# The odd mixer's 31-tap convolution: two of its four channel chunks on TensorE, and the LayerNorm between the output products

## The chip, the cores and the metric

The kernel runs on one core of a Trainium2 chip. The metric is device time in microseconds (us), the median of the timed runs; the profile shows one more execution of the same program, taken by the hardware profiler. The engines are TensorE (PE; its weight loads have rows of their own, PEld), VectorE (DVE), ScalarE (ACT), GpSimd (POOL) and SyncE (SP), whose queue issues the transfers of weights. "Granted clock" is the share of full speed that the chip's throttle gave TensorE.

## The reference

Two layers of a decoder trunk, 512 tokens, 1024 channels, all in float32, each a mixer and a gated ConvFFN with residual sums, then a final norm. The first layer's mixer is the even one (retention and a state-space scan), the second's the odd one, and only the odd mixer is touched:

```python
proj = h @ w_in                                  # h: the normed x, 1024 channels
ca, cg, u = split_cols(proj, [512, 512, 512])
c = ca * sigmoid(cg)                             # GLU
c = causal_dwconv(c, conf_dw_w, conf_dw_b)       # 31 taps, each channel by itself
c = silu(layer_norm(c, conf_ln_g, conf_ln_b))    # over the 512 channels
s = gelu(s5_ssm(u, ...))                         # 32 groups of 16 channels, 64 complex states each
s = s * sigmoid(s @ s5_glu_w)
return concatenate([c, s]) @ w_out               # 1024 -> 1024, added to x
```

## The kernel before

**Tiles.** x lies as 8 chunks of 128 channels (on the partitions) by 512 tokens. A projection to 128 output channels is a loop over the chunks of its input, and each step is three products of 128x512 (`mm3`, L98 to 101): the rounded weight with the rounded input (L99), with the input's remainder (L100), and the weight's remainder with the rounded input (L101). A weight comes through `wload` (L83): a transfer on SP's queue to `wraw` (4 buffers, L88), the rounded copy `whi` on ScalarE (3 buffers, L89), and the remainder `wlo` on VectorE (3 buffers, L90), or on another engine if the caller names one. The input of a projection is split in the same way (L94 on ScalarE, L95 on VectorE). The projections accumulate in one pool of four PSUM banks, all else in a second pool of four. What is not a weight lives in a pool of 56 slots of 128x512.

**Order.** A scheduler orders each engine's instructions by the order in which the program issues them and by what each depends on; `issue_after` and `high_priority` change that in a few places. Each engine runs its own list in order, so an instruction that waits holds up all behind it.

**The odd mixer** (`odd`, L817) issues, in this order:

1. `glu_in(i)`, for the four chunks of convolution channels: the projections pca and pcg (24 products each), on VectorE their products with R (the norm's reciprocal root, L836 and L837), a sigmoid on ScalarE, the gated product, and on ScalarE the first tap with the bias (L842). Of the other 30 taps, `POOLTAPS` gives all of chunk 0 and 20 of chunk 3 to GpSimd, a product and a sum each (L850 and L851), so that chunk 3 has two partial sums.
2. `s5_state(q)`, for the four chunks of S5 channels: the projection pu, whose weight's remainder is made on GpSimd; its product with R (uf, L872); transposes (pu2, puT); the input products pS (L893, 128x64 float32, 16 of them, alternately to the lower and upper 64 partitions); and on VectorE the S5 rotation (L897 to L917), to the states sst.
3. `s5_y(q)`: the output products pY with the kernels `toep` (L931) and `w2` (L933), two banks of PSUM one after the other, both on the lower 64 partitions, and copies on ScalarE (L935). `s5_gelu`: transposes (pyT, L942) and the GELU (L944). `out_loads` brings toep and w2 through SP's queue (L968, L969).
4. The S5 gate: projections pgl, sigmoid, product, split.
5. The output projection over the S5 half, po (8 output chunks of 12 products), each added to x on VectorE (L1010).
6. The taps that are left to VectorE (`conv`, L861): 30 each for chunks 2 and 1, 10 for chunk 3. The scheduler puts them wherever VectorE's list has room. Then the partial sums of chunk 3 are added.
7. The LayerNorm over channels: transposes of the convolution to tokens on the partitions (pLN, L1024), statistics (L1025), root and scaling (ln, L1039 and L1041), transposes back (pLNT, L1046), SiLU (lnc, L1048), split.
8. The output projection over the convolution half, po again (L1056 adds it to x), and with it the next norm's sums.

Of the kernel before, what the change touches and what calls it, by code (L numbers as in the profile page):

```python
# [15 lines left out]
P = 128  # L16
# [9 lines left out]
NPAIR = SH // 2  # L26
POOLTAPS = {0: range(1, 31), 3: range(11, 31)}
WV0 = (0, 1, 3, 6)
# [7 lines left out]
class Trunk:  # L36
# [21 lines left out]

    # ---------------------------------------------------------------- helpers
    def unpack(self, name, items, eng):  # L60
# [108 lines left out]

    # ---------------------------------------------------------------- ConvFFN  # L170
    def ffn(self, l, st, nxt, aside=None, out=None):
# [41 lines left out]
        if out is None:  # L213
            return nst
        # the last channels by halves of the tokens, so that the first half leaves under the second
        c = KC - 1
# [70 lines left out]

    # ---------------------------------------------------------------- even mixer
    def even(self, st):
# [13 lines left out]

        # values of the first head and dt, tokens on the partitions
        mm = nc.tensor.matmul
# [21 lines left out]

        # dt
        bc = lambda t: t.unsqueeze(1).to_broadcast(CH)
# [142 lines left out]

        # retention
        cosR, sinR = self.slot("cosR"), self.slot("sinR")
# [135 lines left out]

    # ---------------------------------------------------------------- S5 parameters
    def s5_prep(self):
# [16 lines left out]
        with self.tc.issue_after(self.dma_mark.ins), self.tc.issue_after(self.add_mark.ins):  # L629
# [87 lines left out]
            cmul(bbr, bbi, b(fr), b(fi), br, bi, bt)  # L717
            # powers by descending exponent: qr[., j] = a^(7-j); the same for a^(8-j)
            pw2_ = self.slot("s5p2")
# [11 lines left out]
            eng.memset(zt, 0.0)  # L731
            # chunk rotation e^(i 8 theta k) and the decay |a|^8
            cur = (co, si)
# [81 lines left out]

    # ---------------------------------------------------------------- odd mixer
    def odd(self, st):  # L817
# [8 lines left out]
        def glu_in(i):  # L826
            pa = self.pp("pca")
            self.proj(pa, ins["wca"][i], xs)
            pg = self.pp("pcg")
            self.proj(pg, ins["wcg"][i], xs)  # L830
            if "R" not in st:
                self.norm_end(st)
            R = st["R"]
            a = self.tp.tile([P, T], F32, name="cp", tag="cp", bufs=2) if i in POOLTAPS else self.slot("ca")
            b = self.tmp("cg")
            V(a, pa, R, op=ALU.mult)  # L836
            V(b, pg, R, op=ALU.mult)  # L837
            nc.scalar.activation(b, b, AF.Sigmoid)
            V(a, a, b, op=ALU.mult)
            cin[i] = a  # L840
            o = self.slot(f"cv{i}")
            nc.scalar.activation(o, a, AF.Identity, scale=kw[:, i, 30:31], bias=kb[:, i:i + 1])  # L842
            cv[i] = o
            pa = o
            if i in POOLTAPS and len(POOLTAPS[i]) < 30:
                pa = self.slot("cvp")
                nc.gpsimd.memset(pa, 0.0)
            for s in POOLTAPS.get(i, ()):
                t = self.tp.tile([P, T], F32, name="prod", tag="prod", bufs=1)
                nc.gpsimd.tensor_scalar(t, a, kw[:, i, 30 - s:31 - s], 1.0, op0=ALU.mult, op1=ALU.mult)  # L850
                nc.gpsimd.tensor_tensor(pa[:, s:], pa[:, s:], t[:, :T - s], op=ALU.add)  # L851
            cvp[i] = pa
# [10 lines left out]

        us, sst = {}, {}

        def s5_state(q):
            p = self.pp("pu")
            self.proj(p, ins["wu"][q], xs, eng=nc.gpsimd)
            if "R" not in st:
# [52 lines left out]
        def s5_y(q):  # L922
            y2 = [self.slot("y2")[:64].rearrange("p (i x) -> p i x", i=4) for _ in range(2)]
            for b in range(2):
                tp_, w2 = outw[q][b]
                p = self.ps("pY")
                for gl in range(4):
                    g = 4 * b + gl
                    ks = slice(g * 64, g * 64 + 64)
                    o = p[:64, gl * P:(gl + 1) * P]  # L930
                    mm(o, lhsT=us[q][:, ks], rhs=tp_.rearrange("p (i g c) -> p i g c", i=8, g=4)[:, :, gl, :],  # L931
                       start=True, stop=False)
                    mm(o, lhsT=sst[q][:, ks], rhs=w2[:, gl * P:(gl + 1) * P], start=False, stop=True)  # L933
                for e in range(2):
                    nc.scalar.copy(y2[e].rearrange("p i (g c) -> p g i c", c=16)[:, 4 * b:4 * b + 4],  # L935
                                   p[:64].rearrange("p (g i c) -> p g i c", g=4, i=8)[:, :, 4 * e:4 * e + 4])
            return y2
# [41 lines left out]
        s5_loads(0)  # L979
        glu_in(1)  # L980
        s5_loads(1)
        s5_state(0)
        s5_state(1)
        s5_loads(2)
        s5_loads(3)
        s5_state(2)
        s5_state(3)
        for q in range(4):
            out_loads(q)
        glu_in(2)  # L990
        y2[0] = s5_y(0)
        glu_in(3)
        for q in range(1, 4):
            y2[q] = s5_y(q)
            s5_split(q - 1)
        s5_split(3)
        mix = [None] * 8
        for m in range(4):
# [7 lines left out]
            mix[4 + m] = (hi, lo)  # L1006
        for c in range(KC):
            p = self.pp("po")
            self.proj(p, ins["woo"][c, :, 4 * P:], mix[4:])
            V(self.x[c], self.x[c], p, op=ALU.add)  # L1010
        conv(2)
        conv(1)
        conv(3, range(1, 4), ev[3])
        conv(3, range(4, 11), ev[4])
        for i in range(4):
            if cvp[i] is not cv[i]:
                V(cv[i], cv[i], cvp[i], op=ALU.add)
        bs, mv = self.small("bs4", [P, NT, 4, 6], 1), self.small("mv", [P, NT, 2])
        pt = [self.ps("pLN") for _ in range(NT)]
        for i in range(4):  # L1020
            with self.tc.issue_after(self.mark.ins), self.tc.high_priority() if i < 3 else nullcontext():
                for t in range(NT):
# [13 lines left out]
        for t in range(NT):  # L1036
# [3 lines left out]
            else:  # L1040
                nc.vector.tensor_scalar(z, pt[t], rs[:, t:t + 1], nm[:, t:t + 1], op0=ALU.mult, op1=ALU.add)  # L1041
            zs.append(z)
        for i in range(4):
            p = self.ps("pLNT")
# [15 lines left out]

# ---------------------------------------------------------------- host layout
def wtiles(w):
    k, m = w.shape
    return w.reshape(k // P, P, m // P, P).transpose(2, 1, 0, 3).reshape(m // P, P, k)


def chunks(v):
    return np.moveaxis(v.reshape(-1, P, *v.shape[1:]), 1, 0)
# [16 lines left out]
def layout(i):  # L1085
# [26 lines left out]
    o["wu"] = wtiles(w[:, 1024:])  # L1112
    o["wgl"], o["woo"] = wtiles(n["o_glu_w"][0]), wtiles(n["o_w_out"][0])
    c["kw"], c["kb"] = chunks(n["o_dw_w"][0].T), chunks(n["o_dw_b"][0])
    c["lg"], c["lb"] = chunks(n["o_ln_g"][0]), chunks(n["o_ln_b"][0])
# [43 lines left out]
```

## Time and profile before

| | |
|---|---|
| timed runs, us | 1402.01, 1399.62, 1400.68; median 1400.68 |
| profiled execution, first to last instruction, us | 1400.0 |
| busy, us (share) | PE 1331.6 (95%), PEld 1104.2 (79%), DVE 991.1 (71%), ACT 547.9 (39%), POOL 299.2 (21%) |
| mean granted clock of TensorE | 0.969 |
| traffic of the transfers | 143.00 MB |

For the profiled execution only its span is given; the timed runs are the measure of the time. The odd mixer lies about from 810 to 1035 us of the span. How to read the rows shown further down: a row of a stretch has its bounds and length, then for each engine in turn the busy time with the count of instructions, the granted clock, the transfers' busy share and GB/s. A group's row has the line, the engine, the operation, the tiles out<-in, shapes, the count, then busy time, the mean length of one in ns, and after a second bar the idle time of the engine just before. A single row begins with its start and its length in us; what stands in square brackets is the engine's idle time before it and what ended that.

### The profile page before, as it was taken

To read this page: it belongs to the slowest core of one execution; us is meant where nothing else is said; L and a number is where in the kernel's file an instruction comes from. 1 tells how busy PE (TensorE), PEld (TensorE's weight loads), DVE (VectorE), ACT (ScalarE), POOL (GpSimd) and SP (SyncE) were. 2 spreads that over 40 slices of the span, in tenths; PEclk is the share of its full clock that TensorE was granted. 3 is DMA by queue.
4 is the path that set the end of the run, shared out by engine and by line. 5 is a ranking of instruction groups with operands and counts; after the bars stand their busy time and mean duration, and the time that the engine had idled before them with its cause. 6 is when DMAs were issued, how large, how long until landed. Compare 5 with 4: busy or idle time off the path is not lost.

```text
span 1400.0 us, 17171 instructions
## 1 busy us (share of the span) xinstructions
PE 1331.6 (95%) x6468; PEld 1104.2 (79%) x6468; DVE 991.1 (71%) x1573; ACT 547.9 (39%) x769; POOL 299.2 (21%) x420
## 2 busy tenths in 40 slices
PE   8999999999999899999999987968799999999997
PEld 7788888888887778888888865756588888888887
DVE  6887777688578998777533369999887777774333
ACT  5455444444353334444322221143444444443221
POOL 0210010002009446800000059769000000000100
PEclk9999999999999999999999997888899999999999
DMA  6432232231244434532333332401142333232321
GB/s 218 153 121 69 75 113 91 90 105 64 90 142 121 124 95 139 177 106 87 98 98 94 106 113 83 143 16 53 62 134 94 103 91 106 90 97 88 102 75 61
DMA packets 48803, 143.00 MB, mean 102 GB/s; under 512 B 6352, under 2 KB 7680, under 8 KB 48720
## 3 DMA queue, kind: packets, MB, share of 16 engines
q1 hardware_dynamic: 42560, 124.34, 28.0%
q0 software_dynamic: 5872, 17.37, 4.3%
q8 instruction: 51, 0.84, 0.2%
q14 instruction: 32, 0.26, 0.1%
q10 hardware_dynamic: 288, 0.19, 0.0%
HBM read 131.88 MB, written 9.99 MB: 101 GB/s over the span
## 4 chain that ended last, share of the span: by engine, by line
PE 78%; DVE 17%; issue 2%; POOL 2%; ACT 1%; DMA 0%; DVEq 0%; ACTq 0%; POOLq 0%
PE pup L101 10%; PE pup L99 10%; PE pup L100 10%; PE pdn L101 6%; PE pdn L99 6%; PE pdn L100 6%; DVE cv L861 3%; DVE wlo L90 3%; PE po L99 2%; PE po L101 2%; PE po L100 2%; DVE ffa L189 1%; PE pxbc L100 1%; PE pxbc L99 1%; PE pxbc L101 1%
## 5 line engine op out<-in xcount | busy, mean ns | idle before, releaser
L89 ACT CAST whi<-wraw 128x1024 fp32r<-128x1024 f32 (+3 forms) x246 | 231.0, 940 | 492.5 <-PE pup L100 131.5
L90 DVE TENSOR_TENSOR wlo<-wraw,whi 128x1024 fp32r<-128x1024 f32 (+3 forms) x242 | 272.7, 1128 | 137.6 <-ACT whi L89 137.5
L101 PE MATMUL pup<-xh,wlo 128*128 128x512 f32 x704 | 276.1, 392 | 9.0 <-DVE wlo L90 9.0
L99 PE MATMUL pup<-xh,whi 128*128 128x512 f32 x704 | 276.5, 393 | 0.0
L100 PE MATMUL pup<-xl,whi 128*128 128x512 f32 x704 | 275.2, 391 | 0.0
L101 PEld LDWEIGHTS pup<-xh,wlo 128*128 128x128 f32 x704 | 133.1, 189 | 38.2 <-DVE wlo L90 10.1
L100 PEld LDWEIGHTS pup<-xl,whi 128*128 128x128 f32 x704 | 133.2, 189 | 27.7
L99 PEld LDWEIGHTS pup<-xh,whi 128*128 128x128 f32 x704 | 133.2, 189 | 27.3
L189 DVE SCALAR_TENSOR_TENSOR ffa<-ffh,c,ffa 128x511 f32<-128x511 f32 (+1 forms) x176 | 149.8, 852 | 2.9
L99 PE MATMUL pdn<-acth,whi 128*128 128x512 f32 (+1 forms) x374 | 140.9, 377 | 0.0
L100 PE MATMUL pdn<-actl,whi 128*128 128x512 f32 (+1 forms) x374 | 140.8, 377 | 0.0
L101 PE MATMUL pdn<-acth,wlo 128*128 128x512 f32 (+1 forms) x374 | 140.8, 377 | 0.0
L184 DVE TENSOR_TENSOR ffh<-pup,R 128x512 f32<-128x512 f32 x88 | 60.5, 687 | 63.6 <-PE pup L101 63.3
L231 POOL TENSOR_SCALAR x<-x,c 128x512 f32<-128x512 f32 (+1 forms) x9 | 9.3, 1034 | 402.0 <-ACT acc L127 302.9
L186 ACT ACTIVATE ffa<-ffh,c 128x512 f32<-128x512 f32 x88 | 71.9, 817 | 49.5 <-DVE ffh L184 47.3
L100 PEld LDWEIGHTS pdn<-actl,whi 128*128 128x128 f32 x374 | 70.4, 188 | 12.9
L101 PEld LDWEIGHTS pdn<-acth,wlo 128*128 128x128 f32 x374 | 70.4, 188 | 12.9
L99 PEld LDWEIGHTS pdn<-acth,whi 128*128 128x128 f32 x374 | 70.4, 188 | 12.8
L100 PE MATMUL po<-ml,whi 128*128 128x512 f32 x192 | 76.5, 399 | 3.8 <-DVE ml L95 3.8
L99 PE MATMUL po<-mh,whi 128*128 128x512 f32 x192 | 76.2, 400 | 0.5 <-ACT mh L94 0.5
L101 PE MATMUL po<-mh,wlo 128*128 128x512 f32 x192 | 76.3, 397 | 0.1
L94 ACT CAST acth<-ffg 128x512 fp32r<-128x512 f32 x44 | 27.3, 621 | 106.7 <-DVE ffg L196 104.4
(424 smaller groups left out, 2436.3 us busy)
## 6 DMA issues: line engine op xcount, KB each, us to landing
wraw<-in_wup_dram SPq DMA_DIRECT2D x88, 512.0 KB, 3.5
wraw<-in_wdn_dram SPq DMA_DIRECT2D x32, 512.0 KB, 3.5
wraw<-in_weo_dram SPq DMA_DIRECT2D x32, 256.0 KB, 3.0
wraw<-in_wxbc_dram SPq DMA_DIRECT2D x12, 512.0 KB, 3.7
wraw<-in_wdn_dram SPq DMA_DIRECT2D x16, 384.0 KB, 3.1
wraw<-in_wz_dram SPq DMA_DIRECT2D x8, 512.0 KB, 3.4
wraw<-in_wg_dram SPq DMA_DIRECT2D x8, 512.0 KB, 3.7
ar<-acd POOLq DMA_DIRECT2D x16, 256.0 KB, 4.0
```

Source lines behind the costliest of these rows:

```text
L89: nc.scalar.copy(hi[:, :n], raw[:, :n])
L90: (eng or nc.vector).tensor_tensor(lo[:, :n], raw[:, :n], hi[:, :n].bitcast(F32), op=ALU.subtract)
L94: self.nc.scalar.copy(hi, src)
L99: mm(out, lhsT=w[0], rhs=x[0], start=start, stop=False)
L100: mm(out, lhsT=w[0], rhs=x[1], start=False, stop=False)
L101: self.mark = mm(out, lhsT=w[1], rhs=x[0], start=False, stop=stop)
L184: nc.vector.tensor_tensor(h, p, st["R"], op=ALU.mult)
L186: nc.scalar.activation(a, h, AF.Identity, scale=dw[:, j, 2:3], bias=db[:, j:j + 1])
L189: nc.vector.scalar_tensor_tensor(a[:, s:], h[:, :T - s], dw[:, j, tap:tap + 1], a[:, s:], op0=ALU.mult, op1=ALU.add)
L231: self.nc.gpsimd.tensor_scalar(self.x[c][:, ts], self.x[c][:, ts], st["g"][:, c:c + 1], 1.0, op0=ALU.mult, op1=ALU.mult)
L861: nc.vector.scalar_tensor_tensor(a[:, s:], cin[i][:, :T - s], kw[:, i, 30 - s:31 - s], a[:, s:], op0=ALU.mult, op1=ALU.add)
```

## The change

The convolution's chunks 2 and 3 move to TensorE. With taps j = 0, 2, ... 30 as 16 shifts, one product takes two taps: its input `cx` holds 64 channels of the gated product on one half of the partitions and the same channels, one token later, on the other half; its weight `kd` has the two taps on two diagonals of 64x64. A chunk is two halves g of 64 channels, so 32 products, which the code issues with the halves alternating, each half to its own 64 partitions of one bank (pcv). The copy that is one token late is made on ScalarE, and ScalarE adds the bias when it takes the result from PSUM. The kernels come from a new input array through SP's queue. Chunk 0 stays on GpSimd and chunk 1 on VectorE; GpSimd loses its 20 taps of chunk 3 and the remainders of the pu weights, which go to VectorE.

Beside that the order changes: glu_in(1) stands behind the first s5_state; glu_in(2) and glu_in(3) stand ahead of the S5 outputs, with the loads of the convolution kernels and of toep and w2 around them; the convolution of chunk 2 stands ahead of the first S5 output, that of chunk 3 behind the last. The S5 output products of both halves go to one PSUM bank, alternating. The LayerNorm's transposes and statistics stand behind the first two of the eight S5 output chunks, and its transposes back behind all eight. In lines of the kernel after, `wload` and `mm3` stand one line lower (L89 to L91, L100 to L102).

```diff
-POOLTAPS = {0: range(1, 31), 3: range(11, 31)}
+POOLTAPS = {0: range(1, 31)}
+PECONV = (2, 3)
...
             V(b, pg, R, op=ALU.mult)
             nc.scalar.activation(b, b, AF.Sigmoid)
+            if i in PECONV:
+
+                x2 = [self.slot("cx") for _ in range(2)]
+                for g in range(2):
+                    own, oth = slice(64 * g, 64 * g + 64), slice(64 - 64 * g, 128 - 64 * g)
+                    V(x2[g][own], a[own], b[own], op=ALU.mult)
+                    nc.vector.memset(x2[g][oth, 0:1], 0.0)
+                    nc.scalar.copy(x2[g][oth, 1:], x2[g][own, :T - 1])
+                cin[i] = x2
+                return
...
+        def conv_loads(i):
+            for h in range(4):
+                t = self.slot("kd")
+                ld(t, ins["kd"][PECONV.index(i), :, h * T:(h + 1) * T])
+                kd.setdefault(i, []).append(t)
+
+        def conv_pe(i):
+
+            p = self.ps("pcv")
+            for j in range(16):
+                s = 2 * j
+                for g in range(2):
+                    w = kd[i][j // 4][:, (j % 4) * P + 64 * g:(j % 4) * P + 64 * g + 64]
+                    mm(p[64 * g:64 * g + 64, s:], lhsT=w, rhs=cin[i][g][:, :T - s], start=j == 0, stop=j == 15)
+            cv[i] = cvp[i] = self.slot(f"cv{i}")
+            nc.scalar.activation(cv[i], p, AF.Identity, bias=kb[:, i:i + 1])
...
-            self.proj(p, ins["wu"][q], xs, eng=nc.gpsimd)
+            self.proj(p, ins["wu"][q], xs)
...
+            p = self.ps("pY")
+            for gl in range(4):
+                for step in range(2):
+                    for b in range(2):
...
+                        o = p[64 * b:64 * b + 64, gl * P:(gl + 1) * P]
...
         glu_in(0)
         s5_loads(0)
-        glu_in(1)
         s5_loads(1)
         s5_state(0)
+        glu_in(1)
...
         s5_state(3)
+        for i in PECONV:
+            conv_loads(i)
+        glu_in(2)
         for q in range(4):
             out_loads(q)
-        glu_in(2)
+        glu_in(3)
+        conv_pe(2)
         y2[0] = s5_y(0)
-        glu_in(3)
         for q in range(1, 4):
             y2[q] = s5_y(q)
             s5_split(q - 1)
         s5_split(3)
+        conv_pe(3)
+        conv(1)
...
+        out_s5(range(2))
         bs, mv = self.small("bs4", [P, NT, 4, 6], 1), self.small("mv", [P, NT, 2])
         pt = [self.ps("pLN") for _ in range(NT)]
-        for i in range(4):
-            with self.tc.issue_after(self.mark.ins), self.tc.high_priority() if i < 3 else nullcontext():
+        with self.tc.issue_after(self.mark.ins):
+            for i in (2, 3, 0, 1):
...
+        out_s5(range(2, KC))
         for i in range(4):
             p = self.ps("pLNT")
```

How this moves the instructions stands in three places. First TensorE where the last gate projection (pcg of chunk 3) ends, before:

```order
L100 MATMUL pcg<-xl,whi 128x512
L101 MATMUL pcg<-xh,wlo 128x512
L931 MATMUL pY<-toep,us 64x128
L933 MATMUL pY<-w_7622,sst 64x128
L931 MATMUL pY<-toep,us 64x128
```

and after (pcv is the convolution of chunk 2; "x2" are the two halves):

```order
L101 MATMUL pcg<-xl,whi 128x512
L102 MATMUL pcg<-xh,wlo 128x512
L891 MATMUL pcv<-cx,kd 64x512 x2
L891 MATMUL pcv<-cx,kd 64x510 x2
...
L891 MATMUL pcv<-cx,kd 64x484 x2
L891 MATMUL pcv<-cx,kd 64x482 x2
L964 MATMUL pY<-toep,us 64x128 x2
L967 MATMUL pY<-w_7705,sst 64x128
L967 MATMUL pY<-w_7709,sst 64x128
L964 MATMUL pY<-toep,us 64x128 x2
```

The 32 products of chunk 2 stand between the last gate projection and the first S5 output, whose products now alternate.

Second, VectorE around the remainder of the last gate weight (wlo 128x1024), before (cv_7187 is chunk 1; a tap with a shift of s tokens has 512 - s columns):

```order
L904 SCALAR_TENSOR_TENSOR s5rot<-rho,s5rot 128x256
L90 TENSOR_TENSOR wlo<-wraw,whi 128x1024
L908 TENSOR_TENSOR s5rot<-s5rot,rot 128x256
...
L837 TENSOR_TENSOR cg<-pcg,R 128x512
L90 TENSOR_TENSOR wlo<-wraw,whi 128x512
L861 SCALAR_TENSOR_TENSOR cv_7187<-ca,c_447,cv_7187 128x494
```

and after (cv_7294 is chunk 1):

```order
L935 SCALAR_TENSOR_TENSOR s5rot<-rho,s5rot 128x256
L849 MEMSET cx 64x1
L91 TENSOR_TENSOR wlo<-wraw,whi 128x1024
L939 TENSOR_TENSOR s5rot<-s5rot,rot 128x256
...
L840 TENSOR_TENSOR ca<-pca,R 128x512
L841 TENSOR_TENSOR cg<-pcg,R 128x512
L875 SCALAR_TENSOR_TENSOR cv_7294<-ca,c_447,cv_7294 128x504
L91 TENSOR_TENSOR wlo<-wraw,whi 128x512
L848 TENSOR_TENSOR cx<-ca,cg 64x512 x2
```

Before, 17 of chunk 1's taps stand ahead of that remainder (the next is the 18th, 494 columns), after, 7 do; the input of the convolution, cx, follows close behind the last product with R.

Third, TensorE at the LayerNorm, before (cv_7019 is chunk 0, cv_7713 chunk 2, cv_7807 chunk 3):

```order
L100 MATMUL po<-ml,whi 128x512
L101 MATMUL po<-mh,wlo 128x512
L1024 MATMUL pLN<-c_106,cv_7019 128x128 x4
L1024 MATMUL pLN<-c_106,cv_7187 128x128 x3
L1024 MATMUL pLN<-c_106,cv_7713 128x128 x3
...
L1024 MATMUL pLN<-c_106,cv_7807 128x128
L1046 MATMUL pLNT<-c_106,ln 128x128 x16
L99 MATMUL po<-mh,whi 128x512 x3
```

and after (cv_7844 is chunk 2, cv_8031 chunk 3):

```order
L101 MATMUL po<-ml,whi 128x512
L102 MATMUL po<-mh,wlo 128x512
L1061 MATMUL pLN<-c_106,cv_7844 128x128 x4
L100 MATMUL po<-mh,whi 128x512
...
L1061 MATMUL pLN<-c_106,cv_8031 128x128
L101 MATMUL po<-ml,whi 128x512
...
L102 MATMUL po<-mh,wlo 128x512
L1084 MATMUL pLNT<-c_106,ln 128x128 x16
L100 MATMUL po<-mh,whi 128x512 x3
```

The 16 transposes of the LayerNorm, which stood between the last S5 output product and the transposes back, now stand behind two of the eight output chunks, all but four of them among the products of the third; the 72 products of the other six chunks stand between the first of those transposes and the transposes back.

More of the change, by code (lines that the diff above doesn't have):

```diff
@@ L833, in glu_in @@
             R = st["R"]
-            a = self.tp.tile([P, T], F32, name="cp", tag="cp", bufs=2) if i in POOLTAPS else self.slot("ca")
+            if i in PECONV:
+                a = self.tmp("ca")
+            else:
+                a = self.tp.tile([P, T], F32, name="cp", tag="cp", bufs=2) if i in POOLTAPS else self.slot("ca")
             b = self.tmp("cg")
@@ L838, in glu_in @@
             nc.scalar.activation(b, b, AF.Sigmoid)
+            if i in PECONV:
+                x2 = [self.slot("cx") for _ in range(2)]
[6 more added lines that the diff above has]
+                return
             V(a, a, b, op=ALU.mult)
@@ L862, in conv @@
                                                    op0=ALU.mult, op1=ALU.add)
-        us, sst = {}, {}
+        def conv_loads(i):
[12 more added lines that the diff above has]
+            nc.scalar.activation(cv[i], p, AF.Identity, bias=kb[:, i:i + 1])
+        us, sst, kd = {}, {}, {}
         def s5_state(q):
             p = self.pp("pu")
-            self.proj(p, ins["wu"][q], xs, eng=nc.gpsimd)
+            self.proj(p, ins["wu"][q], xs)
             if "R" not in st:
@@ L923, in s5_y @@
             y2 = [self.slot("y2")[:64].rearrange("p (i x) -> p i x", i=4) for _ in range(2)]
-            for b in range(2):
[L925 to L933, printed above, removed]
+            p = self.ps("pY")
+            for gl in range(4):
+                for step in range(2):
+                    for b in range(2):
+                        tp_, w2 = outw[q][b]
+                        g = 4 * b + gl
+                        ks = slice(g * 64, g * 64 + 64)
+                        o = p[64 * b:64 * b + 64, gl * P:(gl + 1) * P]
+                        if step == 0:
+                            mm(o, lhsT=us[q][:, ks],
+                               rhs=tp_.rearrange("p (i g c) -> p i g c", i=8, g=4)[:, :, gl, :], start=True, stop=False)
+                        else:
+                            mm(o, lhsT=sst[q][:, ks], rhs=w2[:, gl * P:(gl + 1) * P], start=False, stop=True)
+            for b in range(2):
                 for e in range(2):
                     nc.scalar.copy(y2[e].rearrange("p i (g c) -> p g i c", c=16)[:, 4 * b:4 * b + 4],
-                                   p[:64].rearrange("p (g i c) -> p g i c", g=4, i=8)[:, :, 4 * e:4 * e + 4])
+                                   p[64 * b:64 * b + 64].rearrange("p (g i c) -> p g i c", g=4, i=8)[:, :, 4 * e:4 * e + 4])
             return y2
@@ L1006, in odd, with out_s5 @@
             mix[4 + m] = (hi, lo)
[L1007 to L1014, printed above, removed]
-        for i in range(4):
-            if cvp[i] is not cv[i]:
-                V(cv[i], cv[i], cvp[i], op=ALU.add)
+        def out_s5(cs):
+            for c in cs:
+                p = self.pp("po")
+                self.proj(p, ins["woo"][c, :, 4 * P:], mix[4:])
+                V(self.x[c], self.x[c], p, op=ALU.add)
+        out_s5(range(2))
         bs, mv = self.small("bs4", [P, NT, 4, 6], 1), self.small("mv", [P, NT, 2])
         pt = [self.ps("pLN") for _ in range(NT)]
-        for i in range(4):
-            with self.tc.issue_after(self.mark.ins), self.tc.high_priority() if i < 3 else nullcontext():
+        with self.tc.issue_after(self.mark.ins):
+            for i in (2, 3, 0, 1):
                 for t in range(NT):
@@ L1113, in layout @@
     o["wgl"], o["woo"] = wtiles(n["o_glu_w"][0]), wtiles(n["o_w_out"][0])
+    k = np.zeros((4, 2, 64, 16, 2, 64), np.float32)
+    taps = np.concatenate([n["o_dw_w"][0][::-1], np.zeros((1, 512), np.float32)]).reshape(16, 2, 4, 2, 64)
+    r = np.arange(64)
+    for g in range(2):
+        for half in range(2):
+            k[:, half, r, :, g, r] = taps[:, half ^ g, :, g, :].transpose(2, 1, 0)
+    o["kd"] = k.reshape(4, P, 2048)[list(PECONV)]
     c["kw"], c["kb"] = chunks(n["o_dw_w"][0].T), chunks(n["o_dw_b"][0])
```

## The prediction

> **What bounds the kernel now.** I read first the page's chain, then the odd mixer in stretches, then the groups of instructions in each stretch, and last the single rows that price the new work. All lines and L numbers are of the kernel before; the profiled span is 1400.0 us, the median of the timed runs 1400.68, so I add 0.7 to a span. The order of instructions differs only between the first input projection of the odd mixer and its last output projection, so the question is when that last projection starts. First the stretches (columns: sum, then PE, weight load, VectorE, ScalarE, GpSimd busy; granted clock; DMA):
>
> ```profile
> 816.00:904.00 88.00, 73.64 (x424) 57.75 (x423) 75.99 (x94) 18.01 (x32) 77.19 (x63) 0.81 0.35 116
> 904.00:985.00 81.00, 62.81 (x301) 49.99 (x300) 80.68 (x94) 30.54 (x53) 54.13 (x41) 0.85 0.12 42
> 985.00:1008.00 23.00, 13.54 (x57) 10.25 (x56) 16.77 (x50) 7.18 (x12) 0.00 (x0) 0.70 0.12 38
> ```
>
> VectorE is busy 80.7 of 81 us from 904 to 985, while TensorE is idle for 18 and runs at 0.85 clock; from 985 to 1008 comes the LayerNorm, with TensorE idle for 9.5. The groups of VectorE, of the first stretch, of 904 to 990 and of 904 to 921, then of GpSimd in the first stretch, say with what:
>
> ```profile
> L861 DVE SCALAR_TENSOR_TENSOR cv<-ca,c,cv 128x511 f32<-128x511 f32 (+16 forms) x17 | 21.3, 1254 | 1.2 <-ACT cv L842 0.9
> L90 DVE TENSOR_TENSOR wlo<-wraw,whi 128x1024 fp32r<-128x1024 f32 x4 | 7.0, 1755 | 0.0
> ...
> L861 DVE SCALAR_TENSOR_TENSOR cv<-ca,c,cv 128x494 f32<-128x494 f32 (+29 forms) x43 | 41.6, 996 | 0.2
> L861 DVE SCALAR_TENSOR_TENSOR cv<-cp,c,cv 128x511 f32<-128x511 f32 (+9 forms) x10 | 11.9, 1188 | 0.0
> ...
> L861 DVE SCALAR_TENSOR_TENSOR cv<-ca,c,cv 128x494 f32<-128x494 f32 (+14 forms) x15 | 10.3, 731 | 0.1
> ...
> L851 POOL TENSOR_TENSOR cv<-cv,prod 128x511 f32<-128x511 f32 (+29 forms) x30 | 40.2, 1342 | 2.4
> L850 POOL TENSOR_SCALAR prod<-cp,c 128x512 f32<-128x512 f32 x30 | 29.3, 978 | 9.0 <-DVE cp L839 6.3
> ```
>
> Seventy taps of the convolution cost VectorE 74.8 us. A tap takes 1.25 us while GpSimd works beside it and 0.73 while it doesn't.
>
> **The price of a product on TensorE.** The change removes 40 taps from VectorE (all 30 of chunk 2, the 10 that chunk 3 had there) and 20 from GpSimd, and adds 64 products: for each chunk 16 shifts, for each shift one product per half of 64 channels, contracted over all 128 partitions. The shifts leave 512, 510, ... 482 columns, 7952 in all for one half. The rows that price them are the S5 input products (pS, 64 columns, halves alternating as in the new code) and its output products (pY, 128 columns, always the same half); "x2" or "x32" counts two records per product:
>
> ```profile
> 911.13 0.38 PE L933 MATMUL pY<-w,sst 128*64 128x128 f32 x2
> 911.35 0.38 PE L931 MATMUL pY<-toep,us 128*64 128x128 f32 x2
> ...
> 924.10 0.63 PE L933 MATMUL pY<-w,sst 128*64 128x128 f32 x2
> 924.53 0.63 PE L931 MATMUL pY<-toep,us 128*64 128x128 f32 x2
> ...
> 858.10:860.00 1.90, 1.90 (x33) 1.79 (x32) 1.90 (x3) 0.00 (x0) 1.82 (x2) 0.50 0.00 0
> ...
> 858.11 1.98 PE L893 MATMUL pS<-us,w 128*64 128x64 f32 x32
> 860.01 0.75 PE L99 MATMUL pu<-xh,whi 128*128 128x512 f32 x1
> ...
> 887.55 1.15 PE L893 MATMUL pS<-us,w 128*64 128x64 f32 x32
> 888.63 0.50 PE L100 MATMUL pca<-xl,whi 128*128 128x512 f32 x1
> ```
>
> A pY product starts every 0.218 us (1.70 ns a column), at half clock every 0.43. If the halves take turns, one chunk is 2 x 7952 x 1.70 = 27.1 us. But pS, at half clock, needs 1.90 us for 16 products where turns would need 16 x 64 x 3.4 ns = 3.4: a factor of 0.55. At full clock it needs 1.08 against 1.74, 0.62, with the change of kind at both ends in it. So products of different halves overlap. The new products are eight times as wide, so fixed parts weigh less: I take 0.53, **14.4 us a chunk**, between 13.5 (perfect overlap) and 16.8 (0.62).
>
> A rule of the Trainium skill speaks against it: "TensorE: Matmul & The Clock Gate", Part 3, The mechanism, says that weight loads overlap running products only when the row group differs, and here both halves use all rows. By its figure (columns / 1.2 ns) 128 loads of 64 columns would be an estimated 6.8 us more. The trace disagrees: pS holds 32 loads and 32 products in 1.08 us.
>
> **Up to the first convolution product.** The split of the last gate weights (pcg of glu_in(3)) is the last thing on VectorE for which the projections wait:
>
> ```profile
> 902.05 2.00 DVE L90 TENSOR_TENSOR wlo<-wraw,whi 128x1024 fp32r<-128x1024 f32 x1
> 903.97 0.41 DVE L908 TENSOR_TENSOR s5rot<-s5rot,rot 128x256 f32<-128x256 f32 x1
> ...
> 906.74 0.69 DVE L837 TENSOR_TENSOR cg<-pcg,R 128x512 f32<-128x512 f32 x1
> ...
> 810.48 2.38 DVE L115 TENSOR_SCALAR rs_i<-rs_v 128x4 int32<-128x4 int32 x1
> ...
> 823.41 0.39 PE L101 MATMUL pcg<-xh,wlo 128*128 128x512 f32 x1
> 823.63 0.39 PE L99 MATMUL pcg<-xh,whi 128*128 128x512 f32 x1
> ```
>
> It ends at 904.0. In the new order 7 instead of 17 taps of chunk 1 stand ahead of it (-10 x 1.25 = -12.5); 3 more weight splits do, as those of wu come back from GpSimd (+3 x 1.76 = +5.3); the 2.38 us of rs_i, long only because GpSimd splits a weight beside it, shrink to the 0.2 of its neighbours, and one split moves in (-1.1). VectorE's idle time there is 88 - 76 = 12 us and I take 1.7 less: each weight has one of three buffers, so a split waits for the product that frees its buffer, and VectorE stands behind it. That gives 894.0. Then the 24 gate products (0.227 each, 5.4) end before the input of the convolution is there: the rest of the S5 rotation 4.4 (2.8 alone, as above, more as GpSimd ends about then), two products with R 1.2, a tap and a split 1.4, the first half of the gated product 0.6, two shifted copies on ScalarE 1.2, and 1.0 of hops between engines: 9.8, so the first convolution product starts at 903.8. TensorE has been idle for 4 us by then. What that does stands at 916.9, where it idles 6.5 us:
>
> ```profile
> 923.62 0.69 PE L931 MATMUL pY<-toep,us 128*64 128x128 f32 x2 [6.52 <-ACT y L935]
> ...
> 928.75 0.43 PE L933 MATMUL pY<-w,sst 128*64 128x128 f32 x2
> ```
>
> It stays at half clock for 5 us, a loss of 2.5. Convolution of chunk 2: 14.4 + 2.5, to 920.7. Its kernel loads (8 x 256 KB) go out ahead of it on SP's queue, and the 16 loads of toep and w2 now stand behind them and behind the first output weights, whose buffer is free at about 901:
>
> ```profile
> 878.07 0.33 SPq L968 DMA_DIRECT2D toep<-tpd  x1
> 887.64 0.32 SPq L969 DMA_DIRECT2D w<-w2d  x1
> ```
>
> They took 10 us to issue, so they land by 914: hidden by the convolution; if it were not there, the S5 outputs would wait for them some 10 us.
>
> **From there to the end of the mixer.** The S5 outputs wait in a row for ScalarE:
>
> ```profile
> 922.95 1.15 ACT L935 COPY y<-pY 64x256 f32<-64x256 f32 x4
> 924.12 1.28 ACT L944 ACT_TABLE_LOAD   x1
> 925.42 1.11 ACT L944 ACTIVATE sg<-pyT 128x512 f32<-128x512 f32 x1
> 926.56 0.62 ACT L94 CAST sh<-sg 128x512 fp32r<-128x512 f32 x1
> ```
>
> Two rounds of pY 4.2, a round of copies 1.15, the table 1.28, GELU and cast 1.65, copies 1.15, GELU and cast 1.65, the split 0.8, three products and one set of transposes 1.3: **13.2 us** until chunk 3's convolution starts, at 933.9. It ends at 948.3. Chunk 1's 30 taps end on VectorE near 920 (21 left at 0.73), chunk 0 on GpSimd near 897: both hidden.
>
> After that TensorE is the bound: 42 pgl products 9.5, 96 po products 21.8, 16 pLN transposes 2.4 (0.60 for four, below), 2.3 of waits (the last gate needs sigmoid, table load, cast, split): **36 us**, to 984.3. LayerNorm's statistics and scaling, 13.9 us before from the first transposes to pLNT, end 6 us ahead of that under the po products, though on VectorE they stand in line with three additions that wait for those.
>
> ```profile
> 985.54 0.60 PE L1024 MATMUL pLN<-c,cv 128*128 128x128 f32 x4
> 999.41 3.71 PE L1046 MATMUL pLNT<-c,ln 128*128 128x128 f32 x16 [4.31 <-ACT ln L1039]
> ...
> 1007.97 0.69 DVE L1056 TENSOR_TENSOR x<-x,po 128x512 f32<-128x512 f32 x1 [1.50 <-PE po L101]
> ```
>
> From pLNT to the first finished output of the last projection it took 8.6 us; with TensorE at full clock I take 7.6, so 991.9 instead of 1008.0: **16.1 us less**. Span 1383.9, time **1384.6**. S5's pY in alternating halves and one PSUM tile is in the 4.2; the smaller edits cost nothing of their own.
>
> **Rivals.** (1) *The halves take turns.* Then each chunk costs 27.1, 12.7 more: 1384.6 + 25.4 = 1410.0, slower. For it: pS is 64 columns wide, and a product of 512 is not in the trace in this form. Against: 1.90 us at half clock. It loses from 22.4 us a chunk upward, 0.83 of the turns. Chance 0.07.
>
> (2) *Weight loads are exposed.* For one, the loads of pY:
>
> ```profile
> L931 PEld LDWEIGHTS pY<-toep,us x64: 133/137/231, 896.1 to 931.6; 128*64 128x64 f32 x64
> ```
>
> 128 loads x 0.137 = 17.5 us: 1402.1, no difference that counts. Against: pS again. Chance 0.03. The rule quoted above is this rival at a lower price.
>
> (3) *The front doesn't shorten.* VectorE, standing behind splits that wait for TensorE while TensorE waits for uf, gives the 10 us back: the last gate weights are ready at 904 as before, 1394.6, still faster. For it: five such waits in the new order; against: VectorE had 12 us idle there before too. Chance 0.10.
>
> My forecast has the remaining 0.80. The range reaches down by perfect overlap (-1.8), no cold start (-2.5) and S5 rotations with less of GpSimd beside them (about -5.5), to 1375, and up to rival 3, 1395, which also holds 0.62 of the turns (+4.8) with a few us of waits not seen; rivals 1 and 2 lie outside. A measurement of this kernel tells about 0.2%, 2.8 us, from no change. Faster 0.90, same 0.03, slower 0.07.
>
> **What would show it.** In the new profile: the 64 records of one chunk's convolution in about 14 to 15 us at full clock (25 or more: rival 1; or visible gaps for loads: rival 2); the first at about 904 (914: rival 3); taps on VectorE at 0.73 from about 897 on, where GpSimd ends; TensorE without a gap from chunk 3's convolution to pLNT, and ln done some us ahead of pLNT. A wait of pY on toep, or pLNT waiting for ln, would be a wait that I have not priced.

## The result and the profile after

The kernel after takes 1375.01 us (median of 4 runs, 1374.28 to 1376.02), the kernel before 1400.49 in runs beside it: a ratio of 0.9817, 95% interval 0.9805 to 0.9829. That is 25.5 us less where 16.1 were forecast, so the direction was right, the measured time lies at the very end of the range (1375.0), and the size was too small. The profiled spans are 1400.0 and 1374.2, so the traces show the same 26 us. One execution each of runs 3 and 11 below, at over 2200 us and a granted clock of 0.556, is left out of their medians.

From about 816 us, where the odd mixer's first gate is ready, to the first finished output of its last projection, the two kernels compare like this, before first, then after (columns as in the stretches above: sum, then PE, weight load, VectorE, ScalarE, GpSimd busy; granted clock; DMA):

```profile
816.00:1008.00 192.00, 149.99 (x778) 117.99 (x777) 173.43 (x235) 55.73 (x97) 131.32 (x104) 0.81 0.23 75
```

```profile
816.00:982.00 166.00, 149.99 (x895) 108.31 (x894) 122.42 (x201) 59.47 (x102) 69.79 (x60) 0.93 0.31 100
```

TensorE has 117 more recorded instructions to do and is busy for the same 150.0 us; it idles for 16.0 us instead of 42.0, and its granted clock is 0.93 instead of 0.81. VectorE loses 51 us of work, GpSimd 62. What TensorE waited for in this part of the program (columns: us in total, times, longest), in the kernel before:

```profile
PE pu L877 <- DVE uf L872: 14.4, 3, 7.2
PE pgl L100 <- DVE slo L95: 7.3, 2, 7.0
PE pY L931 <- ACT y L935: 6.5, 1, 6.5
PE pLN L1024 <- DVE bs L1025: 5.0, 3, 4.1
PE pLNT L1046 <- ACT ln L1039: 4.3, 1, 4.3
PE po L100 <- DVE ml L95: 3.8, 3, 1.9
```

and in the kernel after:

```profile
PE pu L908 <- DVE uf L903: 11.5, 3, 5.9
PE pcv L891 <- ACT cx L850: 3.0, 1, 3.0
PE po L100 <- ACT mh L95: 0.7, 1, 0.7
PE pyT L977 <- ACT y L970: 0.6, 1, 0.6
```

Nearly all waits behind the convolution are gone; what is left is the front, where TensorE waits for uf. The stretches of the kernel after, cut at the points that the prediction named (last gate remainder, first convolution product, its end, chunk 3's start and end, pLNT, first output):

```profile
816.00:888.50 72.50, 60.97 (x382) 48.04 (x381) 62.62 (x86) 19.28 (x33) 63.55 (x55) 0.88 0.34 113
888.50:898.00 9.50, 6.64 (x30) 5.17 (x28) 9.41 (x14) 1.16 (x2) 6.24 (x6) 0.97 0.11 30
898.00:914.50 16.50, 16.36 (x64) 7.41 (x66) 15.86 (x27) 3.70 (x7) 0.00 (x0) 0.81 0.88 301
914.50:928.00 13.50, 12.75 (x173) 10.81 (x169) 5.28 (x8) 11.23 (x23) 0.00 (x0) 1.00 0.01 2
928.00:941.50 13.50, 13.50 (x66) 4.53 (x65) 1.39 (x2) 2.49 (x4) 0.00 (x0) 1.00 0.00 0
941.50:974.60 33.10, 33.10 (x155) 26.87 (x154) 23.78 (x61) 15.89 (x26) 0.00 (x0) 1.00 0.28 81
974.60:982.00 7.40, 6.67 (x38) 5.48 (x37) 4.07 (x7) 5.72 (x10) 0.00 (x0) 1.00 0.22 69
```

Each bound is a row's time in the trace, rounded; the two convolutions and the last gate remainder stand there as

```profile
886.77 1.77 DVE L91 TENSOR_TENSOR wlo<-wraw,whi 128x1024 fp32r<-128x1024 f32 x1
...
898.14 16.89 PE L891 MATMUL pcv<-cx,kd 128*64 128x512 f32 x64 [2.99 <-ACT cx L850]
...
927.99 13.55 PE L891 MATMUL pcv<-cx,kd 128*64 128x512 f32 x64
```

A row's length runs to the end of its last product, which the profile models; the next product on TensorE starts a little earlier, here at 914.50 behind chunk 2. From its first product to the next other one chunk 2 takes 16.4 us.

| point, us | before | predicted | after |
|---|---|---|---|
| last gate remainder ends | 904.0 | 894.0 | 888.5 |
| first convolution product | | 903.8 | 898.1 |
| chunk 2 done | | 920.7 | 914.5 |
| chunk 3 starts | | 933.9 | 928.0 |
| chunk 3 done | | 948.3 | 941.5 |
| transposes back (pLNT) | 999.4 | 984.3 | 974.6 |
| first output added | 1008.0 | 991.9 | 981.9 |

More than half of the 10 us between forecast and measurement is there before the first convolution product; 3 more come between chunk 3 and pLNT.

### The profile page after: what moved, and what is told of

Same layout as the page of the kernel before. It is cut to its first block, busy times and chain, and to the rows that moved or that the text cites. A ratio compares the mean times of both kernels' runs of the same rounds, so it can differ in the third digit from the quotient of the medians.

```text
span 1374.2 us, 17371 instructions
## 1 busy us (share of the span) xinstructions
PE 1333.3 (97%) x6596; PEld 1095.6 (80%) x6596; DVE 939.8 (68%) x1542; ACT 550.3 (40%) x773; POOL 235.2 (17%) x375
## 4 chain that ended last, share of the span: by engine, by line
PE 83%; DVE 11%; issue 2%; ACT 2%; POOL 1%; DMA 0%; DVEq 0%; SPq 0%; ACTq 0%; POOLq 0%
PE pup L100 10%; PE pup L102 10%; PE pup L101 10%; PE pdn L102 6%; PE pdn L101 6%; PE pdn L100 6%; PE po L100 3%; PE po L102 3%; PE po L101 3%; PE pcv L891 2%; DVE wlo L91 2%; DVE ffa L190 1%; PE pxbc L101 1%; PE pxbc L100 1%; PE pxbc L102 1%
## 5 line engine op out<-in xcount | busy, mean ns | idle before, releaser
L91 DVE TENSOR_TENSOR wlo<-wraw,whi 128x1024 fp32r<-128x1024 f32 (+3 forms) x246 | 274.8, 1118 | 157.9 <-ACT whi L90 157.7
L102 PE MATMUL pup<-xh,wlo 128*128 128x512 f32 x704 | 275.9, 392 | 9.2 <-DVE wlo L91 9.2
L100 PE MATMUL pup<-xh,whi 128*128 128x512 f32 x704 | 276.2, 392 | 0.0
L102 PEld LDWEIGHTS pup<-xh,wlo 128*128 128x128 f32 x704 | 133.1, 189 | 38.5 <-DVE wlo L91 10.4
L100 PEld LDWEIGHTS pup<-xh,whi 128*128 128x128 f32 x704 | 133.0, 189 | 27.4
L100 PE MATMUL pdn<-acth,whi 128*128 128x512 f32 (+1 forms) x374 | 140.9, 377 | 0.0
L102 PE MATMUL pdn<-acth,wlo 128*128 128x512 f32 (+1 forms) x374 | 140.8, 377 | 0.0
L100 PEld LDWEIGHTS pdn<-acth,whi 128*128 128x128 f32 x374 | 70.4, 188 | 12.9
L102 PEld LDWEIGHTS pdn<-acth,wlo 128*128 128x128 f32 x374 | 70.4, 188 | 12.8
L100 PE MATMUL po<-mh,whi 128*128 128x512 f32 x192 | 75.2, 393 | 0.7 <-ACT mh L95 0.7
L102 PE MATMUL po<-mh,wlo 128*128 128x512 f32 x192 | 75.5, 393 | 0.0
```

Of the source, the lines that this page charges most:

```text
L91: (eng or nc.vector).tensor_tensor(lo[:, :n], raw[:, :n], hi[:, :n].bitcast(F32), op=ALU.subtract)
L100: mm(out, lhsT=w[0], rhs=x[0], start=start, stop=False)
L102: self.mark = mm(out, lhsT=w[1], rhs=x[0], start=False, stop=stop)
```

## The experiments

Twelve kernels were run, each timed beside the kernel before on the same chip. The ratio given is to that, with its 95% interval; the kernel after has 0.9817.

**1. Halves in turns.**

```diff
-            for j in range(16):
-                s = 2 * j
-                for g in range(2):
+            for g in range(2):
+                for j in range(16):
+                    s = 2 * j
```

> The kernel after, with the 16 products of one half of 64 channels issued before the 16 of the other half, not alternating; the same products and sums. Theory (products to different halves of the output partitions run beside each other, products to the same half take turns): 2 x 7952 columns x 1.70 ns = 27.1 us a chunk at full clock instead of 13.5, so 27 us more, about 1402. Rival (a product of 64 output channels costs half in any order): 13.5 us a chunk, 1375 within 1.5.

1397.95 us, ratio 0.9981 (0.9972 to 0.9991): 22.9 us more than the kernel after. Chunk 3's 32 products in this run:

```profile
938.21 25.32 PE L891 MATMUL pcv<-cx,kd 128*64 128x512 f32 x64
```

25.3 us instead of 13.5: products to different halves of the output partitions run beside each other, and products to the same half take turns. Without the alternation the change would have been worth 2 us. The price of a turn was a little too high: 25.32 us for 2 x 7952 columns are 1.59 ns a column, not 1.70, and 13.5 is 0.53 of it, the factor that the prediction took.

**2. GpSimd's taps left out.**

```diff
-            for s in POOLTAPS.get(i, ()):
+            for s in ():
```

> The kernel after, with GpSimd's 30 taps of chunk 0 left out (that chunk keeps only its first tap), so GpSimd is idle in the odd mixer. Theory A (GpSimd's work makes VectorE's instructions longer, and VectorE sets the front up to the first convolution product): taps of 0.73, splits of 1.23, S5 rotations of about 8 us instead of 13, and the first convolution product 8 to 14 us earlier; time 1361 to 1367. Theory B (the front is set by TensorE and by the weight buffers): VectorE's instructions shorten, but its waits grow by as much; time 1372 to 1375.

1352.36 us, ratio 0.9658 (0.9642 to 0.9674): 22.7 us less than the kernel after, more than either theory allowed. The stretch up to the first convolution product, and that product, in this run:

```profile
816.00:877.50 61.50, 61.20 (x408) 49.01 (x406) 51.33 (x105) 21.24 (x38) 0.00 (x0) 1.00 0.50 160
```

```profile
877.55 13.55 PE L891 MATMUL pcv<-cx,kd 128*64 128x512 f32 x64
```

TensorE is busy for 61.2 of 61.5 us at full clock, so it has become the bound of the front, and the convolution starts without a wait and at full clock. That accounts for the extra gain: theory A counted VectorE's shorter instructions, but not that TensorE's waits for uf (11.5 us in the kernel after, 0.3 here) and chunk 2's time at a lower clock (16.4 us in the kernel after, 13.4 here) go as well. What shortens is seen in the groups of VectorE's instructions, over the front of the kernel after

```profile
L947 DVE TENSOR_TENSOR sst<-s5rot 64x252 f32<-64x252 f32 x6 | 7.3, 1210 | 0.0
L933 DVE TENSOR_TENSOR s5rot<-s5rot 128x256 f32<-128x256 f32 x4 | 5.0, 1260 | 0.0
L935 DVE TENSOR_TENSOR_SCAN s5rot<-rho,s5rot 128x256 f32<-128x256 f32 x4 | 4.4, 1092 | 0.0
L903 DVE TENSOR_TENSOR uf<-pu,R 128x512 f32<-128x512 f32 x4 | 2.7, 672 | 0.0
L928 DVE TENSOR_TENSOR s5rot<-pS,rot 128x256 f32<-128x256 f32 x4 | 1.7, 416 | 0.0
```

and over the front of this run (the number behind the busy time is the mean of one in ns):

```profile
L947 DVE TENSOR_TENSOR sst<-s5rot 64x252 f32<-64x252 f32 x7 | 2.9, 411 | 0.0
L935 DVE TENSOR_TENSOR_SCAN s5rot<-rho,s5rot 128x256 f32<-128x256 f32 x4 | 2.7, 680 | 0.0
L903 DVE TENSOR_TENSOR uf<-pu,R 128x512 f32<-128x512 f32 x4 | 2.7, 676 | 0.0
L928 DVE TENSOR_TENSOR s5rot<-pS,rot 128x256 f32<-128x256 f32 x4 | 1.7, 420 | 0.1
...
L933 DVE TENSOR_TENSOR s5rot<-s5rot 128x256 f32<-128x256 f32 x4 | 1.6, 397 | 0.0
```

These instructions with all inputs in SBUF (sst, the sums and scans of s5rot) take 1.6 to 3.2 times as long beside GpSimd; uf and the rotation's products with pS, which read one input from PSUM, take the same.

**3. LayerNorm behind all S5 output chunks.**

```diff
-        out_s5(range(2))
+        out_s5(range(KC))
...
-        out_s5(range(2, KC))
```

> The kernel after, with the LayerNorm's transposes and statistics behind all eight S5 output chunks, as before the change. Theory (the move hides the chain of statistics, root and scaling): the 13.9 us from the first transposes to the transposes back stand open less the 2.1 that the transposes take anyway, so 11 to 14 us more, 1386 to 1389. Rival (the LayerNorm under the products delays the additions and splits that the products wait for, and gives part of it back): under 6 us more, below 1381.

1382.52 us, ratio 0.9872 (0.9856 to 0.9889): 7.5 us more, between the theory and the rival. The move was worth less than the 11 to 14. In this run pLN starts at 971.4 and pLNT at 979.9, 8.5 us later, and the long wait in between is

```profile
PE pLNT L1083 <- ACT ln L1076: 4.8, 1, 4.8
```

The 13.9 of the kernel before held 4.1 us of TensorE waiting for statistics that stood on VectorE behind the last taps; these taps are gone whichever place the LayerNorm has.

**4. Chunk 1's input at its old place.**

```diff
         s5_loads(0)
+        glu_in(1)
         s5_loads(1)
         s5_state(0)
-        glu_in(1)
```

> The kernel after, with the input of chunk 1 at its old place ahead of the first S5 state; then 15 instead of 7 of chunk 1's taps stand on VectorE ahead of the remainder of the last gate weight. Theory (VectorE sets the front, each tap there moves the end by its length): 8 x 1.2 = 9.6 us more, about 1385. Rival (VectorE's 10 us of idle time in the front take the taps): under 3 us more, below 1378.

1378.46 us, ratio 0.9848 (0.9834 to 0.9863): 3.5 us more, near the rival. The 15 taps ahead of the last gate remainder are 18.8 us of VectorE's time where the 7 of the kernel after are 8.4, so the price of a tap was right. The remainder

```profile
895.02 1.76 DVE L91 TENSOR_TENSOR wlo<-wraw,whi 128x1024 fp32r<-128x1024 f32 x1
```

ends at 896.7, 8.2 us later than in the kernel after: of the 10.4 us of taps, VectorE's idle time took 4.7, and the rotations took 2.3 more. The first convolution product starts only 5.5 later, at 903.6, since what VectorE does behind the remainder is shorter there. Chunk 2 then takes 13.4 us instead of 16.4, as TensorE doesn't wait ahead of it and has a granted clock of 1.00:

```profile
903.63 13.88 PE L891 MATMUL pcv<-cx,kd 128*64 128x512 f32 x64
```

Neither theory had both halves of this.

**5. The pu remainders on GpSimd again.**

```diff
-            self.proj(p, ins["wu"][q], xs)
+            self.proj(p, ins["wu"][q], xs, eng=nc.gpsimd)
```

> The kernel after, with the remainders of the four pu weights on GpSimd again, as before the change. Theory (GpSimd's work and VectorE's lengthen each other, so which of the two makes these remainders matters little): VectorE loses 4 splits (4 x 1.6) and 4 more taps of chunk 1 come ahead of the last gate remainder (4 x 1.2), GpSimd runs 10 us longer beside it, and the root ahead of R takes its 2.4 us again: 1375 to 1380. Rival (GpSimd was late with these remainders and TensorE waited for them): 1382 or more, with TensorE waiting for GpSimd in the waits.

1380.20 us, ratio 0.9851 (0.9836 to 0.9866): 5.2 us more, just above the theory's upper end; TensorE waits for GpSimd nowhere. VectorE's rotations and states (57 instructions, and in the kernel after the first 0.07 us of one more), from 814.2 to the end of the last gate remainder in the kernel after, then to its start in this run (it ends at 896.75, with no rotation in between; columns: sum, VectorE busy on these, clock, DMA):

```profile
814.20:888.54 74.34, 38.66 (x58) 0.89 0.35 115
```

```profile
814.20:894.88 80.68, 42.61 (x57) 0.87 0.33 105
```

What one remainder on GpSimd does to one instruction of VectorE is seen in the kernel before; VectorE, then GpSimd:

```profile
845.99 2.56 DVE L903 TENSOR_TENSOR_SCAN s5rot<-rho,s5rot 128x256 f32<-128x256 f32 x1
```

```profile
845.41 2.59 POOL L90 TENSOR_TENSOR wlo<-wraw,whi 128x1024 fp32r<-128x1024 f32 x1
```

The scan, 0.68 us without GpSimd, takes 2.56 here and ends 0.55 us after GpSimd's remainder, as if most of it had stood behind that. Whether a remainder costs VectorE more than a tap on GpSimd does was not measured by itself.

**6 and 7. All of GpSimd's taps on VectorE.** In the first the scheduler places them, in the second both chunks' first taps are held back until the gate product of chunk 2.

```diff
-POOLTAPS = {0: range(1, 31)}
+POOLTAPS = {}
...
-            V(b, pg, R, op=ALU.mult)
+            gm[i] = V(b, pg, R, op=ALU.mult)
...
-        conv(1)
+        conv(0, after=gm[2])
+        conv(1, after=gm[2])
```

(The first has conv(0) and conv(1) without `after`.)

> The kernel after, with GpSimd's 30 taps of chunk 0 on VectorE; nothing is left out, and GpSimd is idle in the odd mixer. The scheduler puts about 23 instead of 7 taps ahead of the last gate remainder. Theory (GpSimd beside VectorE costs more than the taps are worth; VectorE has 10 us idle in the front without GpSimd and over 30 between the S5 outputs and the LayerNorm): 1352 of the run without the taps, plus 16 x 0.73 = 12 less the 10 idle, 1352 to 1360. Rival (60 taps keep VectorE busy until after the LayerNorm's place): 1370 or more, with the LayerNorm's transposes waiting for taps.

> As the run before it (all 60 taps of chunks 0 and 1 on VectorE, GpSimd idle), and the first tap of either chunk is held back until the gate product of chunk 2, so that no tap stands ahead of the last gate remainder. Theory: the front as in the run without GpSimd's taps or 1 to 2 us shorter; 60 taps x 0.73 = 44 us and 17 us of other work from 870 on end at about 931, when the LayerNorm begins there: 1351 to 1356. Rival (the splits of the S5 outputs queue behind taps on VectorE): 1360 or more.

1352.98 us, ratio 0.9655 (0.9639 to 0.9671), and 1352.19 us, ratio 0.9651 (0.9637 to 0.9666): the whole computation, as fast as the run that left GpSimd's taps out. The two can't be told apart. In the second VectorE's 60 taps take

```profile
L875 DVE SCALAR_TENSOR_TENSOR cv<-ca,c,cv 128x511 f32<-128x511 f32 (+29 forms) x60 | 40.1, 730 | 0.2
```

40.1 us, a start every 0.67, and TensorE's longest waits up to the first output are

```profile
PE po L100 <- ACT mh L95: 0.7, 1, 0.7
PE pgl L101 <- DVE slo L96: 0.6, 1, 0.6
PE pu L908 <- DVE sst L944: 0.3, 1, 0.3
```

This version beats both kernels: 48 us under the kernel before, 23 under the kernel after.

**8. Three chunks on TensorE.**

```diff
-POOLTAPS = {0: range(1, 31)}
-PECONV = (2, 3)
+POOLTAPS = {}
+PECONV = (0, 2, 3)
...
         s5_state(1)
+        conv_pe(0)
```

(and the loads of its kernels ahead of the first S5 state)

> The kernel after, with chunk 0 on TensorE too (three chunks there, chunk 1 on VectorE, GpSimd idle); its 32 products stand behind the second S5 state. Theory: without GpSimd TensorE has no gap left in the front, so 13.5 us come on top of the 1352 of the run without the taps: 1364 to 1368. Rival (TensorE fills waits with them): 1353 to 1360.

1367.37 us, ratio 0.9759 (0.9745 to 0.9774), 15.0 more than without the taps: as expected, with TensorE busy for 61.2 of 61.5 us of the front once GpSimd is idle (run 2). It still beats the kernel after, whose chunk 0 is on GpSimd.

**9. The kernel before without GpSimd.**

```diff
-POOLTAPS = {0: range(1, 31), 3: range(11, 31)}
+POOLTAPS = {}
...
-            self.proj(p, ins["wu"][q], xs, eng=nc.gpsimd)
+            self.proj(p, ins["wu"][q], xs)
...
+        conv(0)
+        conv(1)
         conv(2)
-        conv(1)
-        conv(3, range(1, 4), ev[3])
-        conv(3, range(4, 11), ev[4])
+        conv(3)
```

> The kernel before, with nothing of the odd mixer on GpSimd: its 50 taps and the four pu remainders go to VectorE, so that no chunk is on TensorE and all 120 taps are on VectorE. Theory (GpSimd's 131 us of work from 816 to 1008 cost VectorE about as much as they save it): 120 taps x 0.73 = 88 instead of 75, four splits more (5), rotations, splits and sums shorter by some 25, so VectorE ends 5 to 10 us earlier: 1388 to 1397. Rival (in the kernel before, GpSimd's share was worth having; only the change makes it a burden): 1405 or more.

1372.06 us, ratio 0.9795 (0.9778 to 0.9811): 28 us less, more than twice the most that the theory gave. With no tap on TensorE it can't be told apart from the kernel after: the two intervals overlap. VectorE does all four chunks

```profile
L861 DVE SCALAR_TENSOR_TENSOR cv<-ca,c,cv 128x511 f32<-128x511 f32 (+28 forms) x120 | 80.9, 730 | 1.2 <-ACT cv L842 0.9
```

in 80.9 us, where 70 taps took it 74.8 beside GpSimd. It does become the bound: TensorE waits for the last two chunks' taps before the LayerNorm,

```profile
PE pLN L1024 <- DVE cv L861: 32.3, 2, 23.0
PE pLNT L1046 <- ACT ln L1039: 4.3, 1, 4.3
```

and that is what two chunks on TensorE take away: from 1372.06 to 1352.19, 19.9 us, with GpSimd idle in both and the other edits of the change in the second.

**10 and 12. One chunk on TensorE.** Chunk 2 there, chunk 3 on VectorE; in the tenth run chunk 0 on VectorE too, in the twelfth on GpSimd as in the kernel after.

```diff
-PECONV = (2, 3)
+PECONV = (2,)
...
-        conv_pe(3)
         conv(1)
+        conv(3)
...
-        out_s5(range(2))
+        out_s5(range(5))
...
-            for i in (2, 3, 0, 1):
+            for i in (2, 0, 1, 3):
...
-        out_s5(range(2, KC))
+        out_s5(range(5, KC))
```

> Chunk 2 alone on TensorE, the 90 taps of chunks 0, 1 and 3 on VectorE, GpSimd idle, and the LayerNorm's transposes behind five of the eight S5 output chunks. Theory (with GpSimd idle, the second chunk on TensorE is still needed, since VectorE's taps end too late for the LayerNorm): TensorE has 13.5 us less to do, but VectorE ends its taps near 943 instead of 931, and the 14 us of the LayerNorm behind that stand open: 1355 to 1362. Rival (VectorE's idle time takes the 30 taps): 13 us less than with two chunks on TensorE and GpSimd idle, 1338 to 1345.

1358.67 us, ratio 0.9699 (0.9685 to 0.9714): with 90 taps VectorE is late again, now for the splits that TensorE needs,

```profile
PE pgl L102 <- DVE wlo L91: 7.9, 1, 7.9
PE po L102 <- DVE wlo L91: 4.1, 1, 4.1
```

so the second chunk on TensorE is worth 5.7 us there, against run 6, whose taps are also placed by the scheduler (6.5 against run 7), which is on the theory's side. The LayerNorm's place is moved in the same edit.

> The kernel after, GpSimd with chunk 0 as there, with chunk 2 alone on TensorE, chunk 3's 30 taps on VectorE behind those of chunk 1, and the LayerNorm's transposes behind five of the eight S5 output chunks. Theory (from 897 on VectorE is the engine with room: 53 taps x 0.67 and 17 us of other work end near 950, when TensorE, with 13.5 us less to do, is in the S5 output products): 1362 to 1369, so that the second chunk on TensorE costs time as long as GpSimd makes the front late. Rival (VectorE's taps are late for the LayerNorm or hold up the splits, as when VectorE had 90 taps): 1376 or more.

1375.32 us, ratio 0.9817 (0.9801 to 0.9834): the same as the kernel after, and the theory's 6 to 13 us of gain are not there. Its working had VectorE end in time, but forgot what queues behind the taps: TensorE waits 4.5 us for an output weight's remainder and 2.6 for an S5 split,

```profile
PE po L102 <- DVE wlo L91: 4.5, 1, 4.5
...
PE pgl L101 <- DVE slo L96: 2.6, 1, 2.6
```

and all of TensorE's waits behind the convolution are 9.8 us, against 1.5 in the kernel after. Of the 13.5 us less work, then, 2.8 are left at pLNT (971.8 against 974.6) and 1.9 at the first output (980.0 against 981.9). The rest was not traced. With GpSimd at work and the LayerNorm's place moved with it, the second chunk on TensorE gains and loses nothing that the timed runs show.

**11. The S5 output products as before.** `s5_y` is put back word for word: a PSUM bank for each half, all products on the lower 64 partitions.

> The kernel after, with the S5 output products as before the change: two banks one after the other, all products on the lower 64 partitions. Theory (products of one half take turns, 16 in 3.5 us instead of 2.0, and two rounds stand on TensorE's way between the two convolutions, with copies on ScalarE that start half a round earlier): 2 to 5 us more, 1377 to 1380. Rival (the round of copies, GELU and transposes on ScalarE sets that stretch, and the products are hidden behind it): within 1 us of 1375.

1380.57 us, ratio 0.9861 (0.9842 to 0.9881): 5.6 us more, a little over the theory. Chunk 2's convolution ends at 913.6 and chunk 3's starts at 930.9 in this run, 17.3 us where the kernel after has 13.5:

```profile
913.58:930.92 17.34, 17.34 (x164) 16.31 (x161) 5.49 (x8) 11.34 (x23) 0.00 (x0) 1.00 0.01 2
```

TensorE is busy all that time, so the products in turns are on its way, and ScalarE's round doesn't set this stretch. That is 3.8 of the 5.6 us; the rest was not traced.

## Why the prediction was right in direction and too small

**The bound.** That VectorE sets when the last projection can start, and that the change moves the bound to TensorE, is what the traces show: TensorE is busy for 33.1 of 33.1 us from chunk 3's end to pLNT.

**The price of the products.** 14.4 us a chunk were predicted, 13.5 measured (-0.9), because a turn costs 1.59 ns a column and not 1.70. Rival 1, halves in turns, is ruled out for the order that the change has and shown for the other order. Rival 2 is ruled out too: the 64 weight loads of a chunk lie within its 13.5 us. By the rule of the Trainium skill ("TensorE: Matmul & The Clock Gate", Part 3, The mechanism) that the prediction weighed, by which weight loads overlap running products only when the row group differs, these loads should have stood in the way; the row of 13.55 us disagrees.

**The front.** This is the step that failed: "Up to the first convolution product", with -10.0 us, measured -15.5. Taps were right (-12.5 predicted, -12.9 measured, 21.32 to 8.38 us of VectorE). Splits were +4.1 instead of +5.3, as one took 1.59 us in the mean and not 1.76; the root ahead of R gave -1.4 instead of -1.1, idle time -2.1 instead of -1.7, other products -0.3. The largest miss is a term that the sum put at nothing: the rotations and states, which it left as they were, gave -2.9 (41.54 to 38.66 us). Run 5, which puts the four remainders back on GpSimd, has them at 42.61, so GpSimd's remainders are what had lengthened them, as far as one run shows. The prediction had this only as an end of its range, at -5.5. Rival 3, the front not shortening, is ruled out. That the time lies at the range's lower end is in part luck: of the three things that were to bring it there, the overlap came true, the rotations gave half, and the cold start stayed; what the rest of the front and the stretch behind chunk 3 gave made up for these.

**The cold start.** TensorE waits 3.0 us for the convolution's input, the granted clock is 0.50 for the first 6 us behind that, and chunk 2 takes 16.4 us instead of 13.4: a loss of 3.0, predicted 2.5. Runs 2 and 4, without that wait, have 13.4, and so has run 5 with a wait of 0.9.

**From chunk 3 to pLNT.** This is the second term that was mis-sized: 36 us were predicted, 33.1 measured. Gate products, output products and transposes came out as predicted; the 2.3 us of waits for the last gate, which the sum had added, are not in the trace, where TensorE has no gap there. The stretch of the S5 outputs (13.2 predicted, 13.5 measured) and the one behind pLNT (7.6 and 7.4) were right.

**What it did not ask.** The prediction priced GpSimd's help as given: a tap on VectorE costs 1.25 us beside GpSimd and 0.73 without, and the 30 taps that stay on GpSimd were counted as hidden. The runs show that these cost 22 to 23 us in the kernel after (runs 6 and 7), and GpSimd's share in the kernel before, 50 taps and four remainders, 28 (run 9). So as much as the change gained was to be had by moving GpSimd's work to VectorE alone. How the change's 25.5 us divide among its edits can't be said as a sum: undoing the place of chunk 1's input, the remainders, the LayerNorm's place and the S5 products one at a time costs 3.5, 5.2, 7.5 and 5.6, and each of these figures holds with the others in place.

## What to carry to other kernels

Where two engines share a list of elementwise work, compare the mean length of the same instruction with the neighbour busy and idle before counting its share as help; here 50 of 120 taps and four weight remainders on a second engine made the first slower by more than they were worth. Where products have 64 output channels, try alternating the halves of the output partitions; here that nearly halved their time. Look at the granted clock behind a wait: here removing a wait of 3.0 us would by estimate save 3.0 more, what chunk 2 lost.

## What the runs showed of the hardware

- VectorE beside GpSimd: means of 1260 against 397 ns (s5rot<-s5rot), 1092 against 680 (scan), 1210 against 411 (sst), all with inputs from SBUF alone; 672 against 676 and 416 against 420 with one input from PSUM. The Trainium skill, page "SBUF — State Buffer", section "Who interferes with whom", states that a VectorE instruction with two SBUF inputs contends with a GpSimd instruction that reads SBUF, and that one with at most one SBUF input, outside the two-port performance modes, doesn't; these rows agree. One row stands apart: rs_i, a TENSOR_SCALAR with one input, took 2.38 us beside GpSimd's remainder in the kernel before and 0.17 without it in the kernel after; in which mode it ran the trace doesn't show.
- TensorE: 32 products with 64 output channels in 13.5 us with the halves alternating, 25.3 in turns, both at a granted clock of 1.00.
- TensorE behind a wait: granted clock 0.50 for the first 6 us after 3.0 us of waiting, and no loss after 0.9 us (run 5).
